# Encoder trunk on one core: four instead of three of eight weight pairs in seven block products, with a low part made by an adding transfer

## The chip, the cores and the metric

The kernel runs on one core of a Trainium2 chip. The metric is device time in microseconds (us), the median of the runs; lower is better. On one core five engines work side by side, each with its own in-order queue: TensorE (PE, with its weight loads shown as PEld), VectorE (DVE), ScalarE (ACT), GpSimd (POOL) and SyncE (SP). SP issues the DMAs that bring weights in. SBUF is the on-chip memory that the weights land in, PSUM the banks that matmuls add into.

## What is computed

The input is 256 positions of width 2048 in float32. Layer 0 does a gated convolution and a spatial gating unit side by side, layer 1 a Fourier mixing; after each comes a feed-forward part, and this is what the change is about:

```python
def swiglu(h, w_gate, w_up, w_down):
    return (jax.nn.silu(h @ w_gate) * (h @ w_up)) @ w_down

for layer in range(DEPTH):
    ...                                   # layer 0: convolution and gating; layer 1: Fourier mixing
    h = rms_norm(x, ffn_norm_g[layer])
    x = x + swiglu(h, ffn_w_gate[layer], ffn_w_up[layer], ffn_w_down[layer])
```

`h` is 256 x 2048, `w_gate` and `w_up` are 2048 x 5632, `w_down` is 5632 x 2048, all float32. Two layers mean two feed-forward parts.

## The kernel before

**Parts.** Matmuls run on rounded operands. Each float32 operand is split into a high part (rounded, made by an ACT cast, L130) and a low part (what is left, `x - hi`, made by a DVE subtraction, L131). A product of two split operands is three matmuls: high by high, high by low, low by high. `three` (L416) does this for one block of 128 x 128 activations and 128 x 512 weights; this text calls it a block product.

**Weights.** All weights come in chunks of 128 x 1024 (512 KB) in the order in which they are used. `fetch` issues a chunk's DMA on SP (L139) into one of the RAWS = 5 `raw` slots, `load` makes its parts in the PARTS = 12 `part` slots, and `chunk` hands out the next item after it has called `load` until the items ahead are worth AHEAD = 5 units. A unit is the PE time of two block products. A slot is given out again when the last reader of the tile in it is done, so an engine can stand waiting for a slot.

**Hidden groups.** A feed-forward part has 11 hidden groups of 512 hidden columns, run in two halves of 6 and 5; behind each half comes its product with `w_down`. A hidden group takes the 16 row blocks of `h` in eight pairs. What is done with a pair is written in SEQ, `ccscscsc`. A pair marked `c` takes two chunks, eight block products. A pair marked `s` uses a scheme of the Strassen kind: gate and up weights of two row blocks form a 2 x 2 block matrix, and seven block products of sums and differences do the work of eight. On the side of `h` its sums (`position_forms`, L395 to L411) are made once for a feed-forward part. On the side of the weights they are made in each group, from the two raw chunks of the pair, as four items: `1122` (the single blocks of the first chunk, cast and subtraction), `21` (half a chunk of the second, L153 and L154), `sum` (a DVE addition, L161, then cast and subtraction) and `sum2` (two DVE additions of half size, L166 and L167, then cast and subtraction).

**Behind a group.** After the last `s` pair ACT copies the bank of `p1` (L461) and DVE combines the four shared banks (L462 to L465). `activate` (L474 to L484) and `turned` (transposes on PE, L494, then a cast and a subtraction, L341 and L343) run while the next group is at its first pairs. These tasks are started by `step`, which `chunk` calls after its loads.

**Order.** A scheduler of the framework puts each engine's instructions in order before the run. It keeps close to the order of the program, but lets an instruction that is ready pass one that isn't.

**Memory before the feed-forward part.** `op` tiles of 128 x 512 come from NOP = 53 slots. In layer 0 they also hold the eight convolution inputs `ys` and the four `vg` of the gating unit.

Of the kernel before, what the change touches and what calls it, by code (L numbers as in the profile page):

```python
# [22 lines left out]
F32 = mybir.dt.float32  # L23
# [17 lines left out]
NG = D // GD  # L41
NV = CD // 512
CH = 8
AHEAD = 5
RAWS, PARTS = 5, 12
NOP = 53
HALVES = (6, 5)
SEQ = "ccscscsc"
PARTIAL = 3
NMISC = 3  # L50
PAIRS = 11
OPEN = 5
# [17 lines left out]
_ffn = []  # L70
for _g in HALVES:
    for _c, _ in ORDER * _g:
        _ffn += ["1122", "21", "sum", "sum2"] if _c == "s" else ["w", "w"]
    _ffn += ["w"] * (KD * 4 * _g // CH)
KINDS = (["w"] * ((4 * KD * KC + 2 * KC * KD) // CH) + _ffn + ["w"] * (KD * KD // CH) + _ffn)
UNITS = {"w": 2, "1122": 1, "21": 0.5, "sum": 1, "sum2": 1}
# [14 lines left out]
def trunk(ctx, tc, xT, vec, sgu_gb, sgu_bs, sgu_wT, w, dft_c, dft_s, out):  # L91
# [12 lines left out]
    def op(dt=F32R, shape=(P, 2 * S), name="op"):  # L104

        return acts.tile(list(shape), dt, name=name, tag="op", bufs=NOP)

# [11 lines left out]
    class Weights:  # L119
        def __init__(self):  # L120
            self.loaded, self.fetched, self.ahead, self.ready = 0, 0, 0, []
            self.tick, self.tasks, self.later, self.credit = 0, [], [], 0.0

        def parts_of(self, x, pieces=1):
# [18 lines left out]
        def load(self, pieces=1):  # L143
            kind = KINDS[self.loaded]
            h = slice(0, 512), slice(512, 1024)
            if kind == "w":
                r = self.parts_of(self.fetch(pieces), pieces)
            elif kind == "1122":
                self.pair = self.fetch(), self.fetch()
                r = self.parts_of(self.pair[0])  # L150
            elif kind == "21":
                x, t = self.pair[1], part()
                nc.scalar.copy(t[:, h[0]], x[:, h[1]])  # L153
                nc.vector.tensor_sub(t[:, h[1]], x[:, h[1]], t[:, h[0]].bitcast(F32))  # L154
                r = t,
            elif kind == "sum":

                t = self.sums = raws.tile([P, CH * P], F32, name="raw")
                two = lambda x: x.rearrange("p (o c) -> p o c", o=2)
                b12 = self.pair[1][:, h[0]].rearrange("p (o c) -> p o c", o=1).broadcast_to([P, 2, 512])  # L160
                nc.vector.tensor_add(two(t), two(self.pair[0]), b12)  # L161
                r = self.parts_of(t)
            else:

                t = raws.tile([P, CH * P], F32, name="raw")
                nc.vector.tensor_add(t[:, h[0]], self.sums[:, h[0]], self.pair[0][:, h[1]])  # L166
                nc.vector.tensor_add(t[:, h[1]], t[:, h[0]], self.pair[1][:, h[1]])  # L167
                r = self.parts_of(t)
            self.ahead += UNITS[kind]
            self.loaded += 1  # L170
            self.ready.append((kind, r))
# [23 lines left out]

        def chunk(self):
            while self.loaded < len(KINDS) and (not self.ready or
                                                self.ahead - UNITS[self.ready[0][0]] < AHEAD):
                self.load()
            self.step()  # L200
            kind, r = self.ready.pop(0)
            self.ahead -= UNITS[kind]
            return r
# [209 lines left out]
    def three(acc, x, wt, first, last):  # L413

        for i, (f, e) in enumerate(((0, 0), (0, 1), (1, 0))):
            nc.tensor.matmul(acc, x[f], wt[e], start=first and i == 0, stop=last and i == 2)  # L416

    def hidden_group(norm, flip, before):

        from_ps = lambda n: [ps.tile([P, 2 * S], F32, name="acc") for _ in range(n)]  # L420
        from_misc = lambda n: [bank() for _ in range(n)]
        block = lambda x, b: [x[:, f * S + b * P:f * S + (b + 1) * P] for f in range(2)]
        cs = from_ps(1) + from_misc(3) if flip else from_ps(4)
        shared = None
        ns = 0
        for i, (c, (ka, kb)) in enumerate(ORDER):
            xa, xb = norm.xs[ka], norm.xs[kb]
            if i == 2:
                before()
            if c == "c":  # L430
                for x in (xa, xb):
                    parts = weights.chunk()
                    for b in range(NB):
                        for n in range(2):
                            three(cs[2 * b + n], block(x, b), [t[:, n * 512:(n + 1) * 512] for t in parts],
                                  i == 0 and x is xa, i == len(ORDER) - 1 and x is xb)
            else:
                if shared is None:
                    shared = from_ps(4) if flip else from_ps(1) + from_misc(3)
                p1, q5, r7, v = shared  # L440
                first, last = ns == 0, ns == _s - 1
                ns += 1
                d = [[t[:, j, :] for t in forms[ka]] for j in range(4)]
                w11, w22 = [[t[:, n * 512:(n + 1) * 512] for t in parts_] for parts_ in [weights.chunk()]
                            for n in range(2)]
                three(p1, block(xa, 0), w11, first, last)
                three(cs[1], d[3], w22, False, False)
                t, = weights.chunk()
                three(cs[0], block(xb, 0), [t[:, :512], t[:, 512:]], False, False)
                t1, t3 = [[t[:, n * 512:(n + 1) * 512] for t in parts_] for parts_ in [weights.chunk()]  # L450
                          for n in range(2)]
                three(q5, d[0], t1, first, last)
                three(r7, d[1], t3, first, last)
                t2, t4 = [[t[:, n * 512:(n + 1) * 512] for t in parts_] for parts_ in [weights.chunk()]
                          for n in range(2)]
                three(cs[2], block(xb, 1), t4, False, False)
                three(v, d[2], t2, first, last)
                if last:

                    a, y, z, zq = [op(F32) for _ in range(4)]  # L460
                    nc.scalar.copy(a, p1)  # L461
                    nc.vector.tensor_sub(y, v, a)  # L462
                    nc.vector.tensor_add(z, y, r7)
                    nc.vector.tensor_add(zq, z, q5)
                    nc.vector.tensor_add(y, y, q5)  # L465
                    sums = a, y, z, zq
        return cs, sums
# [32 lines left out]
    def ffn(norm, after, last=False):  # L500
        forms.clear()

        def all_forms():
            for c, (ka, kb) in ORDER:
                if c == "s":
                    yield from position_forms(ka, norm.xs[ka], norm.xs[kb])

        weights.start(all_forms())
        known = []
        for half, n in enumerate(HALVES):  # L510
            hs, h, final = [], [], half == len(HALVES) - 1

            def before():
                if not known:
                    known.append(True)
                    for _ in norm.factors(along=False):
                        pass
                if h:
                    turned(h, hs, not g % 2)
                    h.clear()  # L520

            for g in range(n):
                cs, sums = hidden_group(norm, g % 2, before)
                weights.start(activate(norm, cs, sums, h))
            k = 4 * (n - 1)
            accs = []
            for m in range(PARTIAL):
                if m == PARTIAL - 1:
                    turned(h, hs, True)
                accs.append(product(hs[:k], last=False))  # L530
            for m in range(KD):
                if final and last and m == KD - 1:
                    acc, = products(hs, 1)
                    nc.vector.tensor_add(res[:, m, :], res[:, m, :], acc)
                else:
                    x = residual(m, product(hs[k:], accs[m], first=False) if m < PARTIAL else product(hs))
                if final:
                    after(m, res[:, m, :])

# [79 lines left out]

    ys = []  # L620
    for j in range(KC):
        ys.append(op(F32, (P, S + 2 * PAD)))
        nc.gpsimd.memset(ys[j][:, :PAD], 0.0)
        nc.gpsimd.memset(ys[j][:, PAD + S:], 0.0)

# [4 lines left out]


    vs = [[[op() for _ in range(NV)] for _ in range(2)] for _ in range(NB)]
    vg = [[op(F32) for _ in range(NV)] for _ in range(NB)]
    st = small.tile([P, NB, NV, 6], F32, name="bnst")

    def gate_norm(nb, accs):
# [159 lines left out]
    weights.drain()  # L796

    n2 = Norm("mix1")
    ffn(n1, n2.add)


# [126 lines left out]
def _feed_forward(gate, up, down):  # L928
# [4 lines left out]
    for n in HALVES:  # L933
# [6 lines left out]
                chunks += [np.concatenate([t[:, g] for t in x], axis=1) for x in two]  # L940
        h = down[4 * g0:4 * (g0 + n)].transpose(2, 0, 1, 3)
        k = 4 * (n - 1)
        t = [h[:PARTIAL, :k], h[:PARTIAL, k:], h[PARTIAL:]]
        chunks += list(_chunks(np.concatenate([x.reshape(-1, P, P) for x in t])))
        g0 += n
    return np.stack(chunks)
# [63 lines left out]
```

## Time and profile before

| | |
|---|---|
| runs | 1871.36 us median of 3 (1871.06 to 1872.3) |
| the profiled execution | 1871.74 us, span from first to last instruction 1869.6 us |
| busy share of the span | PE 99%, PEld 85%, DVE 81%, ACT 56%, POOL 1% |
| granted TensorE clock | 0.998 of full speed |
| chain that ended last | PE 95%, DVE 2%, ACT 1%, DMA 1% |
| bytes read from HBM | 347.54 MB, 187 GB/s over the span |

Busy time of PE is not work at its peak, since matmuls are pipelined; what a matmul costs is read from the distance between starts. In the 40 slices of the span DVE stands at 8 and 9 tenths where hidden groups run and at 5 where the products with `w_down` run.

### The profile page before, as it was taken

How to read it: one execution, taken by the hardware profiler on the slowest of the kernel's cores; microseconds unless marked ns; L12 is line 12 of the kernel's file. 1: busy time of each engine (PE TensorE's matmuls, PEld its weight loads, DVE VectorE, ACT ScalarE, POOL GpSimd, SP SyncE). 2: the span in 40 equal slices, each digit the busy share in tenths (PEclk: the TensorE clock that was granted, in tenths of full speed). 3: DMA queues.
4: the chain of work that ended last, by engine and by line, in shares of the span. 5: the costliest groups of instructions: out<-in, count | busy, mean ns of one | idle time of the engine just before them, and what ended most of it. 6: DMA issues, size and time to landing. Idle time of an engine off the chain costs nothing.

```text
span 1869.6 us, 26252 instructions
## 1 busy us (share of the span) xinstructions
PE 1844.9 (99%) x9802; PEld 1584.8 (85%) x9802; DVE 1506.3 (81%) x2017; ACT 1051.5 (56%) x1445; POOL 19.2 (1%) x46
## 2 busy tenths in 40 slices
PE   7999999999999999999999999999999999999997
PEld 7989988888888888888888988888888888888886
DVE  7999969998897557899876678898996558998854
ACT  7988746555554335556554655555554335555542
POOL 1000000000000000000000000000000000000000
PEclk9999999999999999999999999999999999999999
DMA  7544553555556545555655264555556545555652
GB/s 265 180 157 157 177 197 135 182 209 195 198 206 239 182 159 189 180 204 197 241 192 183 76 210 147 192 201 206 205 205 216 186 165 181 192 199 204 240 190 81
DMA packets 98312, 351.38 MB, mean 188 GB/s; under 512 B 11268, under 2 KB 12420, under 8 KB 98184
## 3 DMA queue, kind: packets, MB, share of 16 engines
q1 hardware_dynamic: 97464, 347.73, 53.3%
q10 hardware_dynamic: 720, 1.97, 0.3%
q8 instruction: 77, 1.26, 0.3%
q14 instruction: 51, 0.42, 0.1%
HBM read 347.54 MB, written 2.10 MB: 187 GB/s over the span
## 4 chain that ended last, share of the span: by engine, by line
PE 95%; DVE 2%; ACT 1%; DMA 1%; issue 1%; SPq 0%; POOL 0%; POOLq 0%; DVEq 0%; ACTq 0%
PE acc L416 31%; PE acc L323 24%; PE m L416 16%; PE acc L324 12%; PE acc L333 2%; PE acc L334 2%; PE acc L335 2%; PE acc L670 1%; PE acc L671 1%; PE acc L672 1%; PE m L494 1%; DVE part L131 0%; DMA raw<-in_w 0%; ACT part L130 0%; PE acc L494 0%
## 5 line engine op out<-in xcount | busy, mean ns | idle before, releaser
L130 ACT CAST part<-raw 128x1024 fp32r<-128x1024 f32 (+1 forms) x725 | 749.4, 1047 | 619.3 <-PE acc L323 293.8
L131 DVE TENSOR_TENSOR part<-raw,part 128x1024 fp32r<-128x1024 f32 (+1 forms) x725 | 872.7, 1218 | 259.2 <-ACT part L130 243.2
L323 PE MATMUL acc<-op,part 128*128 128x512 f32 x1900 | 666.3, 396 | 0.5 <-DVE op L343 0.5
L416 PE MATMUL acc<-part,op 128*128 128x512 f32 x2622 | 641.9, 390 | 1.1 <-DVE op L343 1.1
L416 PEld LDWEIGHTS acc<-part,op 128*128 128x128 f32 x2622 | 489.7, 188 | 103.5 <-issue 1.9
L324 PE MATMUL acc<-op,part 128*128 128x256 f32 x1900 | 531.1, 280 | 0.0
L323 PEld LDWEIGHTS acc<-op,part 128*128 128x128 f32 x1900 | 356.2, 188 | 85.0 <-DVE op L343 0.8
L416 PE MATMUL m<-part,op 128*128 128x512 f32 x1404 | 361.3, 390 | 0.4 <-DVE op L343 0.4
L324 PEld LDWEIGHTS acc<-op,part 128*128 128x128 f32 x1900 | 358.5, 189 | 0.5
L416 PEld LDWEIGHTS m<-part,op 128*128 128x128 f32 x1404 | 263.0, 188 | 56.7 <-issue 0.8
L333 PE MATMUL acc<-op,part 128*128 128x256 f32 x404 | 116.9, 290 | 7.8 <-ACT part L130 5.7
L335 PE MATMUL acc<-op,part 128*128 128x256 f32 x404 | 115.1, 287 | 1.3 <-DVE part L131 1.2
L334 PE MATMUL acc<-op,part 128*128 128x256 f32 x404 | 115.6, 287 | 0.0
L161 DVE TENSOR_TENSOR raw<-raw 128x1024 f32<-128x1024 f32 x66 | 80.5, 1220 | 12.6 <-DMA raw<-in_w 12.6
L333 PEld LDWEIGHTS acc<-op,part 128*128 128x128 f32 x404 | 78.7, 195 | 8.3 <-ACT part L130 5.7
L335 PEld LDWEIGHTS acc<-op,part 128*128 128x128 f32 x404 | 78.1, 194 | 1.9 <-DVE part L131 1.9
L334 PEld LDWEIGHTS acc<-op,part 128*128 128x128 f32 x404 | 78.6, 195 | 0.3 <-DVE op L232 0.2
L561 ACT ACTIVATE op<-op,vt 128x256 f32<-128x256 f32 x168 | 71.9, 500 | 0.0
L386 DVE TENSOR_TENSOR l<-acc,res 128x256 f32<-128x256 f32 x90 | 37.8, 421 | 32.7 <-PE acc L324 32.7
L153 ACT CAST part<-raw 128x512 fp32r<-128x512 f32 x66 | 41.1, 623 | 29.7 <-DMA raw<-in_w 9.7
L578 DVE TENSOR_TENSOR op<-op 128x512 f32<-128x512 f32 x80 | 54.0, 688 | 2.2 <-ACT op L561 1.8
L483 ACT ACTIVATE op<-op,is_r 128x512 f32<-128x512 f32 x44 | 31.8, 724 | 42.3 <-DVE op L474 32.5
(152 smaller groups left out, 1085.9 us busy)
## 6 DMA issues: line engine op xcount, KB each, us to landing
raw<-in_w SPq DMA_DIRECT2D x655, 512.0 KB, 3.6
res<-in_xT SPq DMA_DIRECT2D x7, 256.0 KB, 7.9
out<-res ACTq DMA_DIRECT2D x3, 512.0 KB, 2.8
raw<-in_w SPq DMA_DIRECT2D x4, 128.0 KB, 2.9
op<-in_sgu_wT SPq DMA_DIRECT2D x2, 256.0 KB, 5.2
raw<-in_dft_s SPq DMA_DIRECT2D x1, 512.0 KB
res<-in_xT SPq DMA_DIRECT2D x2, 128.0 KB, 2.2
raw<-in_dft_c SPq DMA_DIRECT2D x1, 256.0 KB, 2.6
```

The costliest lines, as they stand in the source:

```text
L130: nc.scalar.copy(hi[:, c], x[:, c])
L131: nc.vector.tensor_sub(lo[:, c], x[:, c], hi[:, c].bitcast(F32))
L153: nc.scalar.copy(t[:, h[0]], x[:, h[1]])
L161: nc.vector.tensor_add(two(t), two(self.pair[0]), b12)
L323: nc.tensor.matmul(acc, wh, x, start=first and k == 0, stop=False)
L324: nc.tensor.matmul(acc[:, :S], wl, x[:, :S], start=False, stop=last and k == len(xs) - 1)
L333: nc.tensor.matmul(acc, wh, x[:, :S], start=k == 0, stop=False)
L334: nc.tensor.matmul(acc, wh, x[:, S:], start=False, stop=False)
L335: nc.tensor.matmul(acc, wl, x[:, :S], start=False, stop=k == len(xs) - 1)
L416: nc.tensor.matmul(acc, x[f], wt[e], start=first and i == 0, stop=last and i == 2)
L561: nc.scalar.activation(t[:, f * S:(f + 1) * S], src, AF.Copy, scale=wc)
L578: nc.vector.tensor_add(sums, sums, t)
```

## The change

SEQ becomes `ccsscssc`: four `s` pairs in each hidden group, in twos. The order inside an `s` pair changes: the single blocks come last. Their high and low parts are made when the pair is fetched: ACT casts the high part, ACT writes its negative into the slot of the low part, and a DMA issued by POOL adds the raw chunk to it. DVE's subtraction for this item is gone. AHEAD becomes 6 from the first feed-forward part on, RAWS 6, PARTS 13, NOP 50. `ys` and `vg` now lie in five `part` slots. In a half of six groups four instead of three partial products are opened.

```diff
-AHEAD = 5
-RAWS, PARTS = 5, 12
-NOP = 53
+AHEAD, AHEAD_FFN = 5, 6
+RAWS, PARTS = 6, 13
+NOP = 50
-SEQ = "ccscscsc"
-PARTIAL = 3
+SEQ = "ccsscssc"
+PARTIAL = lambda n: 3 if n > 3 else 4
...
-        _ffn += ["1122", "21", "sum", "sum2"] if _c == "s" else ["w", "w"]
+        _ffn += ["pair", "21", "sum", "sum2", "1122"] if _c == "s" else ["w", "w"]
...
+            elif kind == "pair":
+                self.pair = self.fetch(), self.fetch()
+                hi, lo = part(), part()
+                nc.scalar.copy(hi, self.pair[0])
+                nc.scalar.activation(lo, hi.bitcast(F32), AF.Copy, scale=-1.0)
+                nc.gpsimd.dma_start(lo, self.pair[0], accum_op=ALU.add)
+                self.single = hi, lo
+                self.loaded += 1
+                return
             elif kind == "1122":
-                self.pair = self.fetch(), self.fetch()
-                r = self.parts_of(self.pair[0])
+                r = self.single
...
-                p1, q5, r7, v = shared
+                q5, r7, v, p1 = shared
...
-                three(p1, block(xa, 0), w11, first, last)
-                three(cs[1], d[3], w22, False, False)
                 t, = weights.chunk()
                 three(cs[0], block(xb, 0), [t[:, :512], t[:, 512:]], False, False)
                 t1, t3 = two()
                 three(q5, d[0], t1, first, last)
                 three(r7, d[1], t3, first, last)
                 t2, t4 = two()
                 three(cs[2], block(xb, 1), t4, False, False)
                 three(v, d[2], t2, first, last)
+                w11, w22 = two()
+                three(p1, block(xa, 0), w11, first, last)
+                three(cs[1], d[3], w22, False, False)
...
-            for m in range(PARTIAL):
+            for m in range(PARTIAL(n)):
...
-        ys.append(op(F32, (P, S + 2 * PAD)))
+        if j % 3 == 0:
+            three_ys = wts.tile([P, 3, S + 2 * PAD], F32, name="part")
+        ys.append(three_ys[:, j % 3, :])
...
-    vg = [[op(F32) for _ in range(NV)] for _ in range(NB)]
+    vg = [wts.tile([P, NV, 512], F32, name="part") for _ in range(NB)]
+    vg = [[t[:, n, :] for n in range(NV)] for t in vg]
...
+    weights.lead = AHEAD_FFN
     ffn(n1, n2.add)
```

## Rows read from the trace of the kernel before

**Rows 1.** The page: PE's share of the span, and the block products' groups.
```profile
PE 1844.9 (99%) x9802; PEld 1584.8 (85%) x9802; DVE 1506.3 (81%) x2017; ACT 1051.5 (56%) x1445; POOL 19.2 (1%) x46
...
L416 PE MATMUL acc<-part,op 128*128 128x512 f32 x2622 | 641.9, 390 | 1.1 <-DVE op L343 1.1
...
L416 PE MATMUL m<-part,op 128*128 128x512 f32 x1404 | 361.3, 390 | 0.4 <-DVE op L343 0.4
```

**Rows 2.** Waits of PE over the span: total us, times, longest.
```profile
PE acc L333 <- ACT part L130: 5.7, 1, 5.7
```

**Rows 3.** Timeline, layer 1: start us, duration us, engine, instructions merged (x).
```profile
1289.37 1.32 PEld L416 LDWEIGHTS m<-part,op 128*128 128x128 f32 x6
...
1290.73 0.64 PEld L416 LDWEIGHTS acc<-part,op 128*128 128x128 f32 x3
```

**Rows 4.** Windows, four hidden groups: length; busy PE, PEld, DVE, ACT, POOL; clock, DMA share, GB/s.
```profile
1229.30:1398.70 169.40, 169.40 (x765) 140.56 (x764) 153.97 (x180) 96.59 (x115) 0.00 (x0) 1.00 0.57 198
```

**Rows 5.** Groups by line, DVE, these four groups: busy us, mean ns, idle before.
```profile
L131 DVE TENSOR_TENSOR part<-raw,part 128x1024 fp32r<-128x1024 f32 x76 | 91.4, 1222 | 14.7 <-ACT part L130 13.7 <-PE acc L416 0.6
L161 DVE TENSOR_TENSOR raw<-raw 128x1024 f32<-128x1024 f32 x12 | 14.6, 1220 | 0.0
L166 DVE TENSOR_TENSOR raw<-raw 128x512 f32<-128x512 f32 x12 | 8.3, 688 | 0.1
...
L154 DVE TENSOR_TENSOR part<-raw,part 128x512 fp32r<-128x512 f32 x12 | 8.2, 684 | 0.0
```

**Rows 6.** Groups by line, ACT, the same four groups.
```profile
L130 ACT CAST part<-raw 128x1024 fp32r<-128x1024 f32 x75 | 77.5, 1053 | 55.4 <-DVE raw L167 17.0 <-DVE raw L161 16.8 <-DMA raw<-in_w 12.0
L153 ACT CAST part<-raw 128x512 fp32r<-128x512 f32 x12 | 7.5, 623 | 5.8 <-PE m L416 2.6 <-PE acc L416 1.6 <-DMA raw<-in_w 1.4
```

**Rows 7.** DMA from 1229 to 1399 us: queue; issues with KB each, us to landing.
```profile
q1 hardware_dynamic: 9210, 33.56, 56.5%
...
raw<-in_w SPq DMA_DIRECT2D x65, 512.0 KB, 4.6
```

**Rows 8.** The page's DMA issues: another transfer, 256 KB each.
```profile
res<-in_xT SPq DMA_DIRECT2D x7, 256.0 KB, 7.9
```

**Rows 9.** Waits of SP from 1229 to 1399 us.
```profile
SPq L139 <- DVE raw L166: 57.9, 12, 6.2
```

**Rows 10.** Timeline, layer 0's feed-forward part, end of a group's last `s` pair.
```profile
425.01 0.69 DVE L166 TENSOR_TENSOR raw<-raw 128x512 f32<-128x512 f32 x1
...
427.21 0.59 ACT L461 COPY op<-acc 128x512 f32<-128x512 f32 x1 [1.55 <-PE acc L416]
427.69 2.00 ACT L130 CAST part<-raw 128x1024 fp32r<-128x1024 f32 x2
...
428.78 3.50 DVE L131 TENSOR_TENSOR part<-raw,part 128x1024 fp32r<-128x1024 f32 x3 [1.26 <-ACT part L130]
...
430.05 0.30 PEld L416 LDWEIGHTS acc<-part,op 128*128 128x128 f32 x2 [0.36 <-DVE part L131]
```

**Rows 11.** Groups by line, DVE, first group of layer 0's feed-forward part: sums of `h`.
```profile
L397 DVE TENSOR_TENSOR op<-op 128x256 f32<-128x256 f32 x6 | 2.3, 419 | 0.0
...
L408 DVE TENSOR_TENSOR op<-op 128x512 fp32r<-128x512 f32 x3 | 2.1, 685 | 0.0
...
L401 DVE TENSOR_TENSOR op<-op 128x128 f32<-128x128 f32 x6 | 1.6, 285 | 0.0
...
L402 DVE TENSOR_TENSOR op<-op 128x128 f32<-128x128 f32 x3 | 0.9, 286 | 0.0
```

**Rows 12.** Timeline before the feed-forward part: two casts in a row.
```profile
249.85 1.05 ACT L130 CAST part<-raw 128x1024 fp32r<-128x1024 f32 x1 [1.73 <-PE acc L323]
...
252.68 1.05 ACT L130 CAST part<-raw 128x1024 fp32r<-128x1024 f32 x1 [1.78 <-PE acc L323]
```

**Rows 13.** Windows, layer 0 before the feed-forward part, columns as in Rows 4.
```profile
100.00:200.00 100.00, 99.99 (x696) 92.78 (x695) 96.39 (x167) 82.37 (x151) 5.76 (x5) 1.00 0.47 164
```

**Rows 14.** Waits of PE from 40 to 310 us.
```profile
PE acc L323 <- DVE op L343: 0.5, 1, 0.5
```

More of the change, by code (lines that the diff above doesn't have):

```diff
@@ L121, in __init__ @@
             self.loaded, self.fetched, self.ahead, self.ready = 0, 0, 0, []
+            self.lead = AHEAD
             self.tick, self.tasks, self.later, self.credit = 0, [], [], 0.0
@@ L197, in chunk @@
             while self.loaded < len(KINDS) and (not self.ready or
-                                                self.ahead - UNITS[self.ready[0][0]] < AHEAD):
+                                                self.ahead - UNITS[self.ready[0][0]] < self.lead):
                 self.load()
@@ L443, in hidden_group, with two @@
                 d = [[t[:, j, :] for t in forms[ka]] for j in range(4)]
-                w11, w22 = [[t[:, n * 512:(n + 1) * 512] for t in parts_] for parts_ in [weights.chunk()]
-                            for n in range(2)]
+                def two():
+                    parts = weights.chunk()
+                    return [[t[:, n * 512:(n + 1) * 512] for t in parts] for n in range(2)]
+                t, = weights.chunk()
+                three(cs[0], block(xb, 0), [t[:, :512], t[:, 512:]], False, False)
+                t1, t3 = two()
+                three(q5, d[0], t1, first, last)
+                three(r7, d[1], t3, first, last)
+                t2, t4 = two()
+                three(cs[2], block(xb, 1), t4, False, False)
+                three(v, d[2], t2, first, last)
+                w11, w22 = two()
                 three(p1, block(xa, 0), w11, first, last)
                 three(cs[1], d[3], w22, False, False)
[L448 to L457, printed above, removed]
                 if last:
@@ L526, in ffn @@
             accs = []
-            for m in range(PARTIAL):
-                if m == PARTIAL - 1:
+            for m in range(PARTIAL(n)):
+                if m == PARTIAL(n) - 1:
                     turned(h, hs, True)
@@ L535, in ffn @@
                 else:
-                    x = residual(m, product(hs[k:], accs[m], first=False) if m < PARTIAL else product(hs))
+                    x = residual(m, product(hs[k:], accs[m], first=False) if m < PARTIAL(n) else product(hs))
                 if final:
@@ L942, in _feed_forward @@
         k = 4 * (n - 1)
-        t = [h[:PARTIAL, :k], h[:PARTIAL, k:], h[PARTIAL:]]
+        m = PARTIAL(n)
+        t = [h[:m, :k], h[:m, k:], h[m:]]
         chunks += list(_chunks(np.concatenate([x.reshape(-1, P, P) for x in t])))
```

## The prediction

> **What bounds the kernel now.** I read the page's shares first, then PE's waits, then the distance between matmul starts, then one stretch of four hidden groups from every engine's side. PE is busy for 99% of the span [rows 1], and its longest wait is the one for the first weights [rows 2]. That alone doesn't say that PE works at its rate, so I look at starts: six weight loads in front of six block-product matmuls take 1290.73 - 1289.37 = 1.36 us [rows 3], 0.2267 us each. A hidden group has 5 x 24 + 3 x 21 = 183 such matmuls, 22 groups have 4026, which is the 2622 + 1404 of the page [rows 1]. 183 x 0.2267 = 41.49 us; a quarter of the four-group stretch is 42.35 us [rows 4], and eight transposes stand in the rest. So in hidden groups PE runs matmul behind matmul, and a matmul that goes is worth its 0.2267 us, as long as the others keep up.
>
> They keep up narrowly. DVE is busy 153.97 of 169.40 us [rows 4], 91%; the rest is mostly its subtractions waiting for ACT casts, 13.7 us [rows 5]. ACT is at 57% [rows 4], with 16.8 + 17.0 us of waits for DVE's weight sums [rows 6]. In layer 0 the margin is gone in places: the subtraction of the last `sum2` starts at 428.78, and PE's weight load at 430.05 has waited 0.36 us for it [rows 10]. The new version therefore has two things to pass: PE's count, and a supply of weight parts with almost no slack.
>
> **The change part by part.**
>
> *Matmuls.* A `c` pair has 24, an `s` pair 21. One more `s` pair a group takes away 3, over 22 groups 66: 66 x 0.2267 = 14.96 us, all on the path. The order inside a pair moves none of them. Opening four partial products instead of three adds none either.
>
> *DVE per group.* Subtractions of full size: before 10 + 3 x 3 = 19 (the 76 of four groups [rows 5]), after 8 + 4 x 2 = 16. One more `s` pair adds one L161, one L166, one L167 (the duration of L166) and one L154. That is -3 x 1.222 + 1.220 + 2 x 0.688 + 0.684 = -0.39 us. DVE has 153.97 / 4 = 38.5 us a group, after it 38.1 us; PE's group goes from 42.35 to 41.67 us. DVE stays at 91%: the room is 3.6 us instead of 3.9 us. So DVE doesn't become the bound by its sum.
>
> *ACT per group.* Casts go from 19 to 24: `c` 8, and four a pair for the high part, its negative, `sum` and `sum2`, plus one more half. The trace has no negating copy; I take the cast's 1.053 us for it [rows 6] (its ends: 0.623 us for half as many columns, and twice the cast). 5 x 1.053 + 0.623 = 5.9 us: 24.1 becomes 30.0 of 41.7 us, 72%. It is hidden as long as ACT uses the gaps in which it now stands for L161 and L167: (16.8 + 17.0) / 12 = 2.8 us an `s` pair, against 2.1 us of new work in it.
>
> *The adding transfer.* No row shows one. In engine time a raw load of the same 512 KB costs 0.565 x 170 / 65 = 1.48 us of all sixteen [rows 7]; that is the low end, since it moves the same bytes. The high end comes from the slowest large row: 256 KB in 7.9 us [rows 8], so 15.8 us for 512 KB from issue to landing, against 4.6 us for a raw load [rows 7]. I take 1.48 us and 4.6 us, from the row of its own size. A group needs 16 raw loads before (10 + 6) and after (8 + 8), 23.7 us; four adding transfers make it 29.6 of 41.7 us. The deadline: the pair is loaded ahead of its `21`, which is six units ahead of PE, 6 x 1.36 = 8.2 us; PE then takes 21, `sum`, `sum2`, 2.5 units or 3.4 us, before it needs the low part; ACT takes 2.1 us for the two copies. That leaves 9.5 us for the transfer, so 4.6 us is hidden with 4.9 us over, 15.8 us would be 6.3 us late. On POOL's queue there is nothing else in the hidden groups but the one small power of a norm, which is wanted only after the first group.
>
> On this the Trainium skill has a rule: "Collectives: The Full Stack", section "The bandwidth ceiling: the fold count and why AG ≠ RS ≠ AR", says that a DMA's addition costs no cycles by itself but reads two sources, so that it moves at half the rate of a copy. By it my estimate for the transfer would be 2 x 1.48 = 2.96 us of engine time and 35.5 of 41.7 us a group, and the sum would stay the same, since the transfers are still hidden; no run here shows it yet.
>
> *Slots.* SP's raw loads wait for slots that DVE frees late, 57.9 us for L166 alone [rows 9]. Raw slots go from five to six, but the first raw chunk of a pair is now held until the adding transfer is done. A pair holds its two single-block parts for all of its other items, and a group takes 8 x 2 + 4 x 7 = 44 parts instead of 41; 13 slots over 41.7 us give each 12.3 us, 12 gave 12.4 us. Even. I cost the slots at nothing; the ends are in the rivals.
>
> *L461.* The copy of `p1` waited 1.55 us for PE, and two casts stood behind it [rows 10]. `p1` now ends 15 matmuls later in the pair, 3.4 us. What is behind it on ACT is the casts of the next items; with six units ahead they are due 8.2 us later. Cost 0, with an upper end of 3.4 us in every group, 75 us, if the copy is put ahead of casts that PE needs first.
>
> *Sums of `h`.* A fourth pair is formed, once for each feed-forward part: 2 x 0.419 + 2 x 0.285 + 2 x 0.286 + 0.685 = 2.67 us of DVE [rows 11] (L403 costs as L402), 5.3 us in all. It falls into the first groups. Between 0 and 5.3 us reach the end; I take 0.6 us, since the parts stand furthest ahead there, behind a product that needs few.
>
> *Layer 0.* Five of 13 `part` slots are taken until the convolution is done, eight are left for weights. Chunks are used every 252.68 - 249.85 = 2.83 us, and there the cast waits for PE to free a slot [rows 12]: 12 slots are six chunks, 17.0 us from cast to end of use; eight are four, 11.3 us. About 3.1 us of this go into making the parts and 2.8 us into their use, so a cushion of 11 us becomes 5.4 us. In this stretch DVE is at 96% and PE still at 100% [rows 13], so DVE's bursts eat the cushion. Between -0.5 us (all that PE waits there now [rows 14]) and 6 us (the lost cushion, once); I take +0.5 us.
>
> **The sum.** -14.96 + 0.6 + 0.5 = -13.9 us. The profiled execution took 1871.74 us (span 1869.6 and 2.1 around it), so 1857.8 us; it lies 0.4 us over the median of the runs, and the forecast is 1857.5 us. Its own range, from the ends of layer 0 and the sums of `h` and a microsecond of small waits less: 1854 to 1867.
>
> **The rivals.**
>
> *A. ACT works the pair in strict order, and the parts come late (slower).* Place: the two `s` pairs in a row. An `s` pair then costs ACT four casts and a half, 4.84 us, plus its wait after the half cast for L154 and L161 (1.91 us) and for what L166 and L167 take over the cast of `sum` (0.32 us): 7.1 us against PE's 21 x 0.2267 = 4.76 us. It falls 2.3 us behind each time; a `c` pair gives back 5.44 - 2.11 = 3.3 us. Over `s s c s s` that is 4 x 2.3 - 3.3 = 5.9 us, less 1.36 us for the unit of lead: 4.5 us. In the six groups of layer 0's first half there is no margin to take it [rows 10], which costs 6 x 4.5 = 27 us and gives 1884.5 us. It decides from 13.9 / 6 = 2.3 us a group. Against it: the order isn't strict. L166 ran at 425.01, in front of subtractions that stand ahead of it in the program [rows 10], and ACT's gaps are as large as the new work. For it: those same gaps were not filled before. Chance 0.20.
>
> *B. The adding transfer fills the DMA engines (slower).* 23.7 + 4a is over PE's 41.7 us from a = 4.5 us, three times a raw load. At a = 5 us a group takes 43.7 us, 2.0 x 22 = 44 us more: 1901 us. For it: nothing shows its cost. Against it: the row of its size is at a third of the limit. Chance 0.10.
>
> *C. The saved time turns into waiting (the change gives nothing).* The supply and not PE sets the group: then 42.35 us stay, and 1871 us. For it: PE already waited for a subtraction [rows 10]. Against it: DVE's work falls with PE's. Chance 0.08.
>
> *D. Layer 0 pays its upper end,* 1863 us. Chance 0.05.
>
> **How the numbers follow.** The forecast has 0.57, A 0.20, B 0.10, C 0.08, D 0.05. About 0.2%, 3.7 us, is what a measurement of this kernel can tell from no change. Faster: the forecast and D, 0.62. Same: C and a small part of A, 0.10. Slower: the rest of A and B, 0.28. The range for 8 in 10 goes from 1853 up to 1885, where B and the dearer half of A are left out.
>
> **What would show it.** Right: 3960 block-product matmuls at 0.2267 us between starts, group length near 41.7 us, DVE near 91% there, the adding transfers landing in under 9.5 us, PE's waits for parts still below a few us. The forecast is wrong if PE's weight loads wait for L131 or for the adding transfer in most groups. A shows as waits of PE on subtractions in the second `s` of two, with ACT's copies in front of the cast of `sum`; B as a DMA share near 1 and casts waiting for raw chunks; C as a group of 42.35 us with PE at fewer matmuls; D as PE waits before 300 us.

## The result: 1.4% slower

The changed kernel takes 1896.41 us (median of 4 runs, 1892.54 to 1902.91) against 1871.83 us before (1871.06 to 1872.79): a ratio of 1.0137, interval 1.0119 to 1.0154. The forecast was 1857.5 us and its range ended at 1885. The runs of before lie within 0.1% of each other here, those of the changed kernel within 0.5%; but 14 runs of before beside later experiments spread over 0.3%, so the spread alone says little.

The page of the changed kernel (profiled execution 1892.54 us, span 1890.8): engines, the two DMA queues that carry the weights, groups by line, and the DMA issues. Line numbers have moved: the block products L416 are now L427, the cast L130 is L131, the subtraction L131 is L132; L154 to L156 are the cast, the negative copy and the adding transfer of a pair.

```profile
PE 1846.7 (98%) x9736; PEld 1573.9 (83%) x9736; DVE 1497.7 (79%) x2053; ACT 1167.8 (62%) x1581; POOL 95.8 (5%) x134
...
q1 hardware_dynamic: 97464, 347.73, 52.6%
q0 software_dynamic: 12672, 46.14, 13.2%
...
L427 PE MATMUL acc<-part,op 128*128 128x512 f32 x2568 | 639.8, 392 | 12.9 <-DVE op L477 11.3
...
L427 PE MATMUL m<-part,op 128*128 128x512 f32 x1392 | 366.5, 393 | 6.6 <-DVE op L354 3.2
...
L156 POOL DMA_DIRECT2D part<-raw x88 | 76.0, 864 | 1311.3 <-ACT part L155 1175.7
...
L155 ACT ACTIVATE part<-part 128x1024 fp32r<-128x1024 f32 x88 | 93.3, 1061 | 6.0 <-PE acc L334 3.4
...
raw<-in_w SPq DMA_DIRECT2D x655, 512.0 KB, 3.8
part<-raw POOLq DMA_DIRECT2D x88, 512.0 KB, 5.4
```

The 66 matmuls are gone: 2568 + 1392 = 3960. The block products' idle time was 1.1 + 0.4 us [rows 1]; it is 12.9 + 6.6 us. The adding transfers land after 5.4 us and take 13.2% of sixteen engines, 0.132 x 1890.8 / 88 = 2.84 us each.

PE's waits in the changed kernel (total us, times, longest):

```profile
PE acc L427 <- DVE op L477: 11.3, 5, 3.4
PE acc L344 <- ACT part L131: 5.7, 1, 5.7
PE m L427 <- DVE op L354: 3.2, 2, 2.0
...
PE m L427 <- DMA part<-raw: 1.6, 2, 1.0
PE acc L427 <- DMA part<-raw: 1.0, 2, 0.6
```

L477 is the last of the four sums at the end of a group's partial products, and the one that frees the PSUM bank of `q5`. L354 is the subtraction behind the transposes of `turned`, some 17 us into the next group, and frees a bank too. Only four waits, 2.6 us, are for an adding transfer. So PE waits for the bookkeeping between groups, not for the new low part.

Four hidden groups of layer 1, as in [rows 4]: the window, then DVE's and ACT's rows of it [rows 5, 6], then SP's waits [rows 9].

```profile
1199.70:1368.70 169.00, 168.71 (x754) 137.73 (x753) 151.78 (x184) 115.76 (x139) 13.79 (x16) 1.00 0.83 248
```
```profile
L132 DVE TENSOR_TENSOR part<-raw,part 128x1024 fp32r<-128x1024 f32 x64 | 77.0, 1220 | 15.0 <-ACT part L131 14.9
L131 ACT CAST part<-raw 128x1024 fp32r<-128x1024 f32 x64 | 66.0, 1051 | 45.2 <-DVE raw L178 27.6 <-DMA raw<-in_w 9.7 <-PE acc L427 5.0
```
```profile
SPq L140 <- DVE part L132: 60.2, 34, 4.8
SPq L140 <- DVE raw L178: 35.3, 8, 5.1
SPq L140 <- DMA part<-raw: 34.3, 8, 6.6
```

Here the four groups take 169.0 us where before they took 169.4 and the forecast had 166.7. DVE is busy 90%, as forecast; the DMA engines went from 0.57 to 0.83; and SP now holds raw loads back until an adding transfer has given its raw slot free.

**Where the time went.** I add up, over the four stretches of hidden groups, the time from the first block-product matmul to 0.2267 us behind the start of the last. Before: 255.8 + 213.0 + 254.4 + 211.8 = 935.0 us. Changed: 260.0 + 219.3 + 254.5 + 218.8 = 952.6 us. Forecast: 935.0 - 15.0 = 920.0 us. So 32.6 us are lost inside the hidden groups, most in the second stretch of each layer. One of these losses, read closely (changed kernel, timeline at the end of a group: start us, duration, engine, instructions merged, wait before it):

```profile
734.98 1.05 ACT L131 CAST part<-raw 128x1024 fp32r<-128x1024 f32 x1 [1.94 <-DMA raw<-in_w]
...
736.24 1.05 ACT L131 CAST part<-raw 128x1024 fp32r<-128x1024 f32 x1 [0.21 <-DMA raw<-in_w]
...
737.55 1.05 ACT L131 CAST part<-raw 128x1024 fp32r<-128x1024 f32 x1 [0.26 <-DMA raw<-in_w]
...
738.82 1.05 ACT L131 CAST part<-raw 128x1024 fp32r<-128x1024 f32 x1 [0.21 <-DMA raw<-in_w]
740.09 1.05 ACT L131 CAST part<-raw 128x1024 fp32r<-128x1024 f32 x1 [0.22 <-DMA raw<-in_w]
741.37 1.05 ACT L131 CAST part<-raw 128x1024 fp32r<-128x1024 f32 x1 [0.23 <-DMA raw<-in_w]
742.33 0.57 ACT L473 COPY op<-m 128x512 f32<-128x512 f32 x1
...
743.60 0.68 DVE L474 TENSOR_TENSOR op<-m,op 128x512 f32<-128x512 f32 x1
...
744.92 1.22 DVE L172 TENSOR_TENSOR raw<-raw 128x1024 f32<-128x1024 f32 x1
...
746.66 0.68 DVE L477 TENSOR_TENSOR op<-op,acc 128x512 f32<-128x512 f32 x1
...
747.39 0.97 PE L427 MATMUL acc<-part,op 128*128 128x512 f32 x3 [2.44 <-DVE op L477]
```

The casts come 1.27 us apart, since each waits for its raw chunk; in the 17 us from 730 the DMA engines are at 0.94 (the windows below). The copy of `p1`, L473, stands behind six such casts, the subtractions and sums of DVE behind the copy, and `q5`'s bank is free only when L477 is through: PE stands 2.44 us. Then the clock (windows, columns as in [rows 4]: behind POOL's come granted clock, DMA share and GB/s):

```profile
730.00:747.00 17.00, 14.95 (x66) 12.04 (x65) 14.89 (x16) 12.18 (x13) 0.86 (x1) 1.00 0.94 326
...
748.00:749.00 1.00, 1.00 (x6) 0.82 (x5) 1.00 (x2) 0.00 (x0) 0.00 (x0) 0.95 1.06 201
749.00:750.00 1.00, 1.00 (x4) 0.81 (x3) 1.00 (x2) 0.00 (x0) 0.00 (x0) 0.50 0.67 127
750.00:751.00 1.00, 1.00 (x4) 0.71 (x4) 1.00 (x3) 0.20 (x1) 0.00 (x0) 0.50 0.01 0
751.00:752.00 1.00, 1.00 (x4) 0.81 (x3) 0.59 (x2) 1.00 (x2) 0.00 (x0) 0.50 0.66 164
```

About 1.5 us after PE starts again it is granted 0.50, the 1.2 GHz level, for over 3 us; eight matmuls in it start 0.427 us apart in place of 0.227. Wait and slow clock together make about 4 us in this group.

Whose bytes fill the DMA engines (q0 the adding transfers, q1 the raw loads; first from 716 to 733 us, then from 733 to 743), and SP's wait from 716 to 748 us:

```profile
q0 software_dynamic: 283, 1.04, 41.6%
q1 hardware_dynamic: 640, 2.36, 38.3%
```
```profile
q1 hardware_dynamic: 1081, 3.91, 99.4%
q0 software_dynamic: 18, 0.01, 0.5%
```
```profile
SPq L140 <- DMA part<-raw: 10.3, 3, 5.1
```

So while the six casts run, hardly a byte of an adding transfer moves: 1.27 us is the pace of raw loads that have the engines to themselves. They are late from before. Up to 733 us two transfers took 41.6% of the engines, and SP waited 10.3 us for raw slots that transfers held; the loads that fell behind then come in one row. That the transfers are the cause is so far a reading of rows; the experiments were to test it.

### The profile page after: what moved, and what is told of

Read it like the earlier page. It is cut to its first block, busy times and chain, and to the rows that moved or that the text cites. A ratio compares the mean times of both kernels' runs of the same rounds, so it can differ in the third digit from the quotient of the medians.

```text
span 1890.8 us, 26674 instructions
## 1 busy us (share of the span) xinstructions
PE 1846.7 (98%) x9736; PEld 1573.9 (83%) x9736; DVE 1497.7 (79%) x2053; ACT 1167.8 (62%) x1581; POOL 95.8 (5%) x134
## 3 DMA queue, kind: packets, MB, share of 16 engines
q0 software_dynamic: 12672, 46.14, 13.2%
## 4 chain that ended last, share of the span: by engine, by line
PE 78%; DVE 7%; DMA 6%; issue 4%; ACT 3%; SPq 0%; POOL 0%; DVEq 0%; POOLq 0%; ACTq 0%
PE acc L334 23%; PE acc L427 20%; PE m L427 12%; PE acc L335 12%; DMA part<-raw 3%; DMA raw<-in_w 3%; PE acc L346 2%; PE acc L344 2%; PE acc L345 2%; DVE part L132 2%; ACT part L131 1%; ACT part L154 1%; PE acc L685 1%; PE acc L686 1%; PE acc L687 1%
## 5 line engine op out<-in xcount | busy, mean ns | idle before, releaser
L132 DVE TENSOR_TENSOR part<-raw,part 128x1024 fp32r<-128x1024 f32 (+1 forms) x659 | 795.1, 1216 | 277.8 <-PE acc L334 136.4
L131 ACT CAST part<-raw 128x1024 fp32r<-128x1024 f32 (+1 forms) x659 | 682.4, 1046 | 525.8 <-PE acc L335 246.8
L427 PE MATMUL acc<-part,op 128*128 128x512 f32 x2568 | 639.8, 392 | 12.9 <-DVE op L477 11.3
L427 PEld LDWEIGHTS acc<-part,op 128*128 128x128 f32 x2568 | 478.6, 188 | 120.3 <-DVE op L477 13.4
L427 PE MATMUL m<-part,op 128*128 128x512 f32 x1392 | 366.5, 393 | 6.6 <-DVE op L354 3.2
L427 PEld LDWEIGHTS m<-part,op 128*128 128x128 f32 x1392 | 262.7, 190 | 67.8 <-issue 4.7
L156 POOL DMA_DIRECT2D part<-raw x88 | 76.0, 864 | 1311.3 <-ACT part L155 1175.7
L172 DVE TENSOR_TENSOR raw<-raw 128x1024 f32<-128x1024 f32 x88 | 107.3, 1219 | 12.9 <-DMA raw<-in_w 12.6
L154 ACT CAST part<-raw 128x1024 fp32r<-128x1024 f32 x88 | 92.3, 1049 | 30.1 <-DMA raw<-in_w 13.5
L155 ACT ACTIVATE part<-part 128x1024 fp32r<-128x1024 f32 x88 | 93.3, 1061 | 6.0 <-PE acc L334 3.4
L165 DVE TENSOR_TENSOR part<-raw,part 128x512 fp32r<-128x512 f32 x88 | 60.5, 687 | 19.6 <-ACT part L164 18.9
L573 ACT ACTIVATE op<-part,vt 128x256 f32<-128x256 f32 x168 | 72.5, 500 | 0.0
```

Source lines behind the costliest of these rows:

```text
L131: nc.scalar.copy(hi[:, c], x[:, c])
L132: nc.vector.tensor_sub(lo[:, c], x[:, c], hi[:, c].bitcast(F32))
L154: nc.scalar.copy(hi, self.pair[0])
L155: nc.scalar.activation(lo, hi.bitcast(F32), AF.Copy, scale=-1.0)
L156: nc.gpsimd.dma_start(lo, self.pair[0], accum_op=ALU.add)
```

## The experiments

All times are medians. The kernel before took 1870.4 to 1873.4 us beside them. Edits are against the changed kernel unless told otherwise.

**e7_no_add: no transfer at all.**
```
-                nc.gpsimd.dma_start(lo, self.pair[0], accum_op=ALU.add)
```


> The changed kernel without the adding transfer; this leaves out part of the computation: the low part of the single blocks is then the negative of the high part. ACT's two copies and all matmuls stay. It shows what the transfer costs altogether. Theory 1 (banks and the chain from p1): little change, 1888 to 1900. Theory 2 (the transfer, by slots or by engines): the loss goes, 1860 to 1872. Theory 3 (two in a row): little change.


1860.88 us, ratio 0.9936 (0.9921 to 0.9951). The hidden stretches sum up to 920.3 us, the forecast's 920.0. PE's waits for the block products are two of 0.5 us, and the casts' waits for raw chunks go from 60.3 us in all (L131, changed kernel) to

```profile
ACT part L131 <- DMA raw<-in_w: 8.0, 11, 1.6
```
So the transfer costs 35.5 us, and all else in the change is worth 11 us net. Another order of the instructions doesn't explain it: PE's is line for line that of the changed kernel, and 1565 of ACT's 1581 instructions stand in the same place. The total of the casts' waits is no measure of the loss, though: the four groups of before had 12.0 us of them [rows 6], those of the changed kernel 9.7, and before lost nothing by it.

**e14_three_no_add: the same with three `s` pairs**, `SEQ = "ccscscsc"`, and `p1` first in the banks.


> Three pairs in seven products, one at a time, bank order p1 first, without the adding transfer (left out of the computation as before). With the transfers this took 1913.5 us. Theory 2 (the transfers are the loss here too): PE's count sets the time, 1872 to 1878. Theory 2c (single blocks last hold two part slots too long, with or without transfers): still over 1890.


1876.34 us: 15.5 us over e7, from which it differs in the bank order too. The matmul term, 14.96 us, stands.

**e16_half: half of the bytes.**
```
-                nc.gpsimd.dma_start(lo, self.pair[0], accum_op=ALU.add)
+                nc.gpsimd.dma_start(lo[:, :512], self.pair[0][:, :512], accum_op=ALU.add)
```


> The changed kernel with half of each adding transfer, 512 of 1024 columns (the other half of the low part stays the negative of the high part: left out of the computation). The waits stay in place, the bytes halve. Theory 2b (share): half of the 35 us, 1872 to 1884. Theory 2d (the time from the copy to the landing): a transfer has a part that doesn't shrink with its bytes, so more than half stays, 1882 to 1895.


1870.70 us (10 runs): half of the bytes bring back 25.7 of the 35.5 us, more than either theory had. ACT's order is here that of the changed kernel throughout, DVE's in 2049 of 2053 places. Half of a transfer also lands sooner, after 4.1 us, so this run doesn't part bytes from held slots. The wait for L477 is still the block products' longest:

```profile
PE acc L427 <- DVE op L477: 4.7, 4, 2.0
```

**e6_add_from_hbm: no raw slot held.** The transfer adds the weights straight from HBM.
```
-                nc.gpsimd.dma_start(lo, self.pair[0], accum_op=ALU.add)
+                nc.gpsimd.dma_start(lo, w[self.fetched - 2], accum_op=ALU.add)
```


> The changed kernel, but the adding transfer reads the chunk from HBM once more instead of from its raw slot. The DMA engines have no less to do, but the raw slot is free when DVE's weight sums have read it. Theory 2a (the transfer hurts because it holds a raw slot: SP waited 61.7 us for it between 710 and 930 us): faster than the changed kernel by 10 us or more. Theory 2b (it hurts by its share of the DMA engines): the same or slower. Theory 1 (banks): the same.


1894.70 us, the same as the changed kernel within the runs. SP's waits for the adding transfer are gone, but nothing is won: the slot is not the whole cause. This version pays in another coin too, its low parts land after 6.9 us and PE waits 11.7 us for them.

**e13_share_only, then e17_share_of_hi: the transfers' share of the DMA engines alone.** Both add into a scratch place in HBM which nobody reads. e13 reads HBM; e17 reads the high part, so that it can't start before that pair's cast:
```
-                nc.gpsimd.dma_start(lo, self.pair[0], accum_op=ALU.add)
+                nc.gpsimd.dma_start(away[self.loaded % 4], hi, accum_op=ALU.add)
```


> The changed kernel with the 88 adding transfers sent elsewhere: source and destination in HBM, so that they hold no slot of SBUF and nobody waits for them; this leaves out part of the computation (the low part of the single blocks stays the negative of the high part). DVE's and ACT's order is nearly that of the run without transfers (1861). Theory 2b (their share of the DMA engines makes raw loads late, and this is the loss): 1885 to 1900. Theory 2d (PE and the slots wait for the low part itself): 1861 to 1868.


2017.30 us, and it tells nothing of the question: nothing held the transfers in place, all 88 were issued in the first 348 us, in front of the norm's power on POOL's queue, for which PE waited 105.0 us.


> The low part is the bare negative copy, as in e7, so the added half of the low part is left out of the result. The 88 transfers are still there, but each now reads the pair's high part and adds it into a scratch place in HBM: it can't start before that pair's cast, so it stands where it stood in the changed kernel, it holds no raw slot, and no multiplication waits for it. If the 34 to 35 us (1896.4 against 1860.9 in e7) are the transfers' share of the 16 DMA engines, through raw loads and casts that come later: 1885 to 1897, with DVE op L477 again ending the longest PE waits. If they come from the raw slot that the transfer holds, or from the low part that lands late: 1861 to 1868.


1887.58 us (1883.57 to 1891.47). The hidden stretches sum up to 939.7 us, 19.4 over e7, where the changed kernel is 32.3 over it. By medians it is 26.7 us over e7; 4.7 us of that are spent before the first hidden group, where only the four first fills of the scratch place are new. So 19 to 22 us, some six tenths, come from such transfers' share of the DMA engines alone, without a held raw slot and without a part to wait for. Its window, DMA rows and waits:

```profile
1200.00:1380.00 180.00, 177.71 (x796) 144.87 (x795) 160.75 (x196) 123.19 (x148) 14.70 (x17) 1.00 0.86 245
```
```profile
raw<-in_w SPq DMA_DIRECT2D x655, 512.0 KB, 4.3
away<-part POOLq DMA_DIRECT2D x88, 512.0 KB, 7.6
```
```profile
PE acc L427 <- DVE op L477: 7.1, 4, 2.8
```

The wait is again the one for L477. This transfer isn't quite the same one: it writes HBM, and takes 0.149 x 1881.8 / 92 = 3.05 us of engine time; the raw loads land after 4.3 us, where they take 3.8 us in the changed kernel and 3.4 us in e7. So it may show more of a share than the changed kernel's transfer has.

**e10_share and e11_hold: the low part not read** (PE reads the high part twice), the transfer from HBM in e10, from the raw slot in e11.
```
-                self.single = hi, lo
+                self.single = hi, hi
```


> The same with the adding transfer reading from the raw slot: all its bytes, the raw slot held until it is done, and PE not waiting for the low part, which it doesn't read (left out of the computation). Theory 2a (raw slot held): near the changed kernel, 1885 to 1900. Theory 2b (share): the same as the run with the source in HBM, and both far over 1861. Theory 2d (PE waits for the low part): 1860 to 1868.


1910.22 and 1899.42 us. No clean test: the unread part's slot is handed on, and ACT's next cast into it waits for the landing, 54.8 us in e10 and 47.3 us in e11, a wait that the changed kernel doesn't have.

**e1_bank: `p1` first in the order of banks**, `p1, q5, r7, v = shared`, as before.


> The changed kernel with one line turned back: the four shared banks are named p1, q5, r7, v again instead of q5, r7, v, p1. In a group of even number the first of them lies in the large pool of banks, from which the next group's first block takes its bank; q5 is freed by the last of the four DVE additions behind the group (L477), p1 by the ACT copy (L473). Theory 1 (the loss is PE standing for that bank): PE's 11.3 us of waits for L477 and the slow clock behind them (about 5 us) go, 1892 to 1903 us become about 1880. Theory 2 (the adding transfer and the raw slots it holds make the parts late): no change, 1892 to 1903. Theory 3 (two seven-product pairs in a row outrun DVE and ACT): little change, the wait shows under another name.


1885.78 us (1882.93 to 1890.98). By medians 10.6 us of the loss hang on which partial product sits in the bank that the next group wants first. In the profile the longest waits of the block products are now for L354, 5.9 + 4.0 us, and L477 has 3.5: the lateness stays and shows elsewhere. The traced execution of e1 was its slowest, 1890.98 us, and loses nearly as much in the hidden stretches as that of the changed kernel, so no trace shows where the 10.6 us are won. **e5_v_first**, another order with a copy of `v` early on ACT, gives nothing:


> The changed kernel with another end of a group: ACT copies v, which PE finishes before the last item, DVE subtracts p1 from the copy in place, and ACT copies p1 beside that; v takes the first of the four shared banks. Nothing else. Theory 1 (the chain from p1 through ACT to the four DVE additions frees the shared banks too late): PE's waits for L477 go, and the time falls below the 1885.8 us of the version with the bank order alone, to about 1875. Theory 2 (the adding transfer delays raw loads, and everything on DVE is late): no better than the bank order alone, 1883 to 1890.


1896.35 us, above both ranges, L354 with 8.8 + 6.5 us.

**e2_dve_low and e4_fourth_only: no transfer, the low part by DVE.** e2 puts `self.single = self.parts_of(self.pair[0])` in place of the copies and the transfer; e4 is the kernel before with `SEQ = "ccsscssc"`.


> The changed kernel, but the low part of the single blocks is made by DVE's subtraction again, at the same place (when the pair is fetched); no adding transfer, no negating copy. DVE then has 4 x 1.22 = 4.9 us more a group, 43.0 us against PE's 41.7. Theory 1 (bank): DVE is later still, so slower than the changed kernel by about 1.3 us a group and more, over 1920. Theory 2 (adding transfer): waits for raw chunks and for the transfer go, faster than the changed kernel, under 1885. Theory 3 (DVE and ACT outrun): slower, 1910 to 1930, since DVE is what lacks.

> The kernel before with the sequence ccsscssc alone: four pairs in seven products, single blocks first, low parts by DVE, lead of five, 5 raw and 12 part slots. PE loses 66 matmuls, 15.0 us; DVE has 43.0 us a group against PE's 41.7. Theory 1 (bank): the order of banks is the old one, so only DVE's excess shows, 22 x 1.3 = 29 us over 1857, about 1886. Theory 2 (adding transfer): no transfer, so at or under the changed kernel, 1870 to 1890. Theory 3 (two in a row outrun DVE): clearly slower than the changed kernel, 1910 to 1940.


1933.11 and 1945.87 us, the second above every range. e2's window and waits:

```profile
1200.00:1380.00 180.00, 170.21 (x743) 136.29 (x742) 168.65 (x204) 100.03 (x123) 0.00 (x0) 0.99 0.52 181
```
```profile
PE acc L423 <- ACT part L131: 29.4, 35, 1.2
PE m L423 <- ACT part L131: 13.2, 16, 1.2
```
Four subtractions of 1.22 us more a group, 4.9 us, are over DVE's room of 3.6 us. DVE doesn't reach 100% (168.65 of 180 us), but it passes its lateness on: in this window ACT's casts wait 25.8 + 17.4 us for DVE's weight sums. With this order, these slots and these leads, a fourth pair needs its subtractions taken from DVE.

**e12_every_other and e18_half_each: half of the low parts by transfer, half by DVE**, with `p1` first. e12 alternates pairs, e18 splits each part:
```
+                nc.gpsimd.dma_start(lo[:, h[0]], self.pair[0][:, h[0]], accum_op=ALU.add)
+                nc.vector.tensor_sub(lo[:, h[1]], self.pair[0][:, h[1]], hi[:, h[1]].bitcast(F32))
```


> The changed kernel with the bank order turned back, and every other pair's low part made by DVE again: two adding transfers a group instead of four, DVE at 38.1 + 2 x 1.22 = 40.5 us of 41.7. Theory 2 (the transfers are the loss, whichever way): half of the 35 us goes, and DVE's closeness gives some back, 1868 to 1880. Theory 3 (DVE is what lacks): slower than the version with the bank order alone, over 1890.

> Whole computation. The first 512 columns of a pair's low part come by negative copy and adding transfer, the other 512 by a subtraction on DVE; p1 is first in the order of the banks, as in e1. If half the bytes take away 26 us, as in e16 (1870.7), and the bank order gives 10 us or what is left of the waits for L477: 1862 to 1869, below the kernel before (1871). If the four half subtractions of 0.6 us (half of a row of 1.2 us), 2.4 us a group on an engine that was busy 90% of a group, make DVE the bound: 1875 to 1890.


1892.88 and 1902.32 us; e18 lies above both its ranges, and I had hoped that it would beat both kernels. The DMA share of its window falls to 0.69 and the wait for L477 is gone from its longest; in their place PE waits for casts and for the transfer:

```profile
PE acc L428 <- DMA part<-raw: 7.1, 10, 2.2
PE m L428 <- ACT part L131: 6.3, 8, 0.9
PE acc L428 <- ACT part L131: 6.1, 20, 0.7
```
The half subtractions took 0.683 us each, 2.7 us of DVE a group, and cost more than the saved bytes gave: e18 is 16.5 us over e1.

**e3_three_pairs and e8_three_bank: the transfer with three pairs**; e8 has `p1` first.


> The changed kernel with the old sequence ccscscsc: three pairs in seven products, one at a time, all else as changed (single blocks last, adding transfer, lead of six, six raw slots, 13 part slots). PE has its 66 matmuls back, +15.0 us; DVE's work falls to 34.9 us a group of 42.35. Theory 1 (bank): the waits for L477 stay at least in part, 1875 to 1885. Theory 2 (adding transfer): three transfers a group instead of four, waits fall by a quarter, 1885 to 1895. Theory 3 (two in a row): all waits go, and PE sets the time again, 1869 to 1873.

> Three pairs in seven products, one at a time, in the changed machinery, as in the run that took 1922 us, with the bank order p1, q5, r7, v turned back. Theory 1 (banks): the 23.8 us of waits for L477 go and with them the slow clock and what follows, 1880 to 1890. Theory 2 (transfer): little change, over 1910. If it still stands far above 1871, putting the single blocks last costs by something else than the bank of q5.


1922.24 and 1913.52 us, e3 above every range. e8 and e14 differ by the transfer alone: 37.2 us, for three transfers a group instead of four. DVE has more room here, and it doesn't help; ACT does the same copies as in e14.

**e9_raws7_parts12 and e15_lead5: slots and lead.** `RAWS, PARTS = 7, 12`; a lead of five units in place of six.


> The changed kernel with seven raw slots instead of six, and twelve part slots instead of thirteen to make room. The time without the adding transfer was 1861, with it 1896; this asks which of its effects costs. Theory 2a (the transfer holds a raw slot, so the next raw load is issued late): faster than the changed kernel, 1870 to 1888. Theory 2b (the transfer's share of the DMA engines slows the raw loads): the same, 1890 to 1903, or slower for the part slot that is gone. Theory 2c (part slots are what lacks): clearly slower, over 1905.

> The changed kernel with a lead of five units in the feed-forward parts instead of six. Theory 2d (the transfer lands too late for PE): slower, by 1.36 us of lead in each group where it matters, 1905 to 1925. Theory 2c (part slots): faster, 1880 to 1890, since the program asks for fewer parts ahead. Theory 2b (share): the same, 1890 to 1903.


1924.59 and 1919.04 us. A part slot less, with a raw slot more, costs 28 us, a unit of lead less 23 us, and both mainly by the wait that the changed kernel just avoids (in e9 11.9 + 11.4 us). e15's waits:

```profile
PE m L427 <- DMA part<-raw: 10.9, 15, 1.9
...
PE acc L427 <- DMA part<-raw: 6.7, 11, 2.3
```

## Why the prediction was wrong

**The step that failed is "The adding transfer", with its sum of nothing.** Its two sizes were low: 2.84 us of engine time where I took 1.48, 5.4 us to landing where I took 4.6. By the rule that the Trainium skill ("Collectives: The Full Stack", section "The bandwidth ceiling: the fold count and why AG ≠ RS ≠ AR") gives for ReduceScatter in a ring, an addition reads two sources and goes at half the rate; 2.84 / 1.48 = 1.92, so this case's trace agrees with it, for a transfer within SBUF against a load from HBM. But the sizes weren't the error: with 2.96 us the prediction kept the same sum. The error was to ask one question of the transfer, whether it meets its own deadline. All but a few do. Counted in the trace from landing to the first matmul that waits for it, the median is 4.2 us to spare, where I had 4.9; six of 88 have less than 0.3 us, among them the four waits of 2.6 us. What I didn't ask was who else uses the DMA engines. The raw loads do, in bursts: beside two transfers they fall behind, then they come in one row, 17 us at a share of 0.94 where the mean is 0.83, and the casts, and with them the in-order queues of ACT and DVE, run late. e7 and e16 show that the transfers do this, and e17 that 19 to 22 of the 35.5 us come by a share of the engines alone.

**"Slots" was costed at nothing, and belongs to it.** Of the 35.5 us, e17 leaves 14 to 16 for the held raw slot, the part that lands late and the fact that e17's transfer isn't the same. No run parts these in its time: e6 frees the slot and lands later, e10 and e11 made a wait of their own. The 34.3 us that SP waits for transfers in four groups is no measure of it, since SP waits for something nearly always. The four stretches of hidden groups tell a little more (us over e7, one traced execution each):

| | layer 0, six groups | layer 0, five | layer 1, six | layer 1, five |
|---|---|---|---|---|
| changed | 6.8 | 11.1 | 3.7 | 10.6 |
| e17 | 4.7 | 4.3 | 4.9 | 5.6 |
| e6 | 13.9 | 7.1 | 6.1 | 6.3 |

In the stretches of five groups, where the changed kernel loses most, no wait of PE for a transfer is listed in it, and 0.2 us in e6. So the late part is not what costs there. Without a held slot 9.9 us (e17) or 13.4 us (e6) are lost there in place of 21.7. That makes some 8 to 12 us for the held slot, an estimate from single traces of transfers that aren't quite the same.

**"Matmuls" was right:** 15.5 us between e14 and e7, 14.7 us between before and e7 in the hidden stretches.

**"DVE per group" and "ACT per group" were right** in count and duration: 64 subtractions in four groups, 90% busy; the negative copy takes 1.061 us where I took 1.053, ACT 115.76 / 4 = 28.9 us a group where I had 30.0.

**"L461" was costed at 0 and is where the loss shows.** The upper end was put down to the copy standing ahead of casts that PE needs. It was the other way round: the copy stood behind six late casts, and the bank of `q5` waited for it. With raw chunks in time (e7) the same order costs nothing, so the bank order is a condition of the loss and not its cause; e1 wins 10.6 us by it.

**"Layer 0"** cost nothing that shows: the first hidden group starts at 307.2 us, before the change at 309.1, so rival D is out. **"Sums of `h`"** fall behind that; in e7 the first hidden stretch is 1.5 us and the third 0.5 us longer than 18 matmuls less would make it, within the 0 to 5.3 us given.

**Left over in e7:** 3.4 us over the forecast. Its stretch between the two layers' hidden groups, 904.8 to 1138.3 us, is 3.4 us longer than before's. There PE stops 2.55 us for the square of a norm (L264), where before it stops 1.49 us, and the clock behind the stop stands at 0.50 for 6.8 us in e7 and stays at 1.00 before. A window within (columns as above):

```profile
1020.00:1026.00 6.00, 6.00 (x28) 6.00 (x29) 2.98 (x9) 2.40 (x8) 1.01 (x1) 0.50 0.61 182
```
That is enough for the 3.4 us; why the stop is longer isn't shown.

**The rivals.** B came nearest, in its number (1901 us) and in naming the DMA engines, but not as a mechanism: it wanted 4.5 us a transfer, a full group of engine time, and 2.84 us, 35.1 of 41.7 us, were enough. A is out: the subtractions of the second `s` are not what PE waits for, and e7 has ACT's full work without loss. C's sign shows, 169.0 / 4 = 42.25 us a group with fewer matmuls, but not its reason: with the same work on DVE and ACT and no transfer, e7 has its hidden stretches at the forecast. The chance of 0.10 for B stood on a mean over a group, and the supply fails in bursts.

No version with the whole computation beats the kernel before; the nearest of four pairs is e1, 1885.78 us.

## What to carry to other kernels

When you add a user to a shared resource, check its own deadline, and then what everyone else on that resource loses in the fullest few microseconds, not on the mean over a period; where an in-order engine is at 90%, a few late inputs come out as a wait in another place, here a PSUM bank. A stretch in which the resource is full shows the catching up; look in front of it for what fell behind. Two cheap experiments tell the size: leave the addition out, and halve it; here half gave back 25.7 of 35.5 us, so the loss doesn't go by the byte.

## What was not expected of the hardware

An adding transfer of 512 KB from SBUF to SBUF took 2.84 us of all sixteen engines, 5.4 us from issue to landing, and 0.86 us of POOL to issue; the raw loads beside it still landed in 3.8 us in the median. A stop of PE of 2.44 us was followed by over 3 us at the lower clock level, which adds 1.6 us. One of 2.38 us, ending at 1590.24 us in the same trace, was followed by none, and one of 1.99 us in e16 was. Idle time alone understates such a loss: of the 32.6 us lost 19.5 are waits at L427 and some 5 are three such stretches of lower clock; the rest lies in gaps between matmuls too short to be listed as waits.
